# A decoder layer on one core: identity matmuls at the start, another order of the down-projection's units, a layer norm's root by tokens, and a planner with two transfer queues

## The chip, the core and the metric

The kernel runs on one core of a Trainium2 chip. The time is device microseconds (us) of one execution. The engines are called as the profile calls them: PE (TensorE, the matmuls) with PEld (its weight loads), DVE (VectorE), ACT (ScalarE), POOL (GpSimd) and SP (SyncE). Each has an instruction stream of its own that is worked off in order. SP and POOL serve here only to issue transfers: SP plain loads and stores, POOL those that add to what is already in the buffer.

## The reference

One layer over 512 tokens of width 1024, in f32, with 256 memory tokens, a feed-forward width of 2816, and a final norm:

```python
h = _rmsnorm(x, norm_mix_g)
gb, gc, v, u, ug, q, p_g = split(h @ w_in)           # widths 1024 each, p_g 3072
y_a = (gb * conv3(gc * v)) @ w_a_out
u = conv31(u * sigmoid(ug)) + conv_b_bias
y_b = silu(layernorm(u, ln_b_g, ln_b_b)) @ w_b_out
y_c = attention(q, rmsnorm(mem) @ w_kv) @ w_att_out  # 4 heads of 256
g = sigmoid(p_g + b_gate)                            # one gate for each branch and channel
x = x + (g[0] * y_a + g[1] * y_b + g[2] * y_c) @ w_o
gt, up = split(conv3(_rmsnorm(x, norm_ffn_g) @ w_up))
x = x + (silu(gt) * up) @ w_down
out = _rmsnorm(x, norm_final_g)
```

The layer norm's variance is the mean over the 1024 channels of the squared, centred values, and its root scales each token.

## The kernel before

**Products.** Each f32 operand is split on the chip into a high half (a cast on ACT, `whi` for weights, line 405) and a low half (the rest, a subtraction on DVE, `wlo`, line 409), and each product is three matmuls: high by high, high by low, low by high. One low half of the merge's weights is made another way: ACT writes the negated high half and POOL adds the weight to it by a transfer (line 422). The names of buffers in the rows carry numbers that only tell them apart.

**Projections.** The in- and the up-projection are done in quads, two by two blocks multiplied with seven products instead of eight. A quad loads four weight blocks u, v, s, r (SP, line 431). Products 1, 2 and 4 use loaded blocks; 5, 6, 7 and 3 use sums of blocks, which POOL forms by accumulating transfers of 512 KB into the buffers s and u once the product that used their older content has been split (line 532, jobs `s5`, `s6`, `s7`, `s3`). The activations have forms of their own for these products (`ft5`, `ft6`, `ft7`, `fb11` and so on, an ACT cast at line 497 and a DVE subtraction at line 502). The matmuls of all quads stand at line 574, and the PE takes them in a fixed order.

**Start.** The memory's keys and values come first (line 794). The PE waits there for the memory's tokens (`mh`, `ml`) and the first weights.

**Layer norm of branch B.** `acc` holds the convolved channels with tokens along the free axis, 512 columns. The squares of the centred values are added into one buffer of two 512-wide halves. Before, these were split in parts, two matmuls with a matrix of 1/1024 gave the variance on all 128 partitions, ACT took the root of 128x512 and DVE its reciprocal (line 1178). Then `lns` multiplies `acc` by it (line 1185), ACT applies the gain and silu (line 1192), and the result is split into `ybh` and `ybl` (lines 1202, 1206) for the merge of branch B.

**Down-projection.** It is again seven products, here named a, b, d, c, e, f, g, over 11 pairs of channels in six units each (five of two pairs and one of one pair). So `a4` is the fifth unit of product a. A unit of two pairs is 12 steps on the PE of 512 columns (lines 364 to 366). The right operands are `z`, the gated up-projection, in forms of which ACT makes the high half `zh` (line 1632) and DVE the low half `zl` (line 1639), one for each two units. The weights are loaded blocks for a and b, sums with a further block for e, and running sums in the buffers `x_sum` (for f) and `y_sum` (for d, c and g). The products a, c, e and g add up in one chain of two PSUM banks, so before the first unit of c, e or g, DVE has read the banks into the rows `x` (`read`, line 1770); b, d and f have banks of their own. The rows `x` are the layer's input to this block, kept in DRAM (`x1_kept`) and loaded again during the down-projection. a0 to a2 stand between the last products of the up-projection.

**Order.** A planner (`Jobs`) emits the instructions. Its job list for the PE is in program order. For ACT, DVE and transfers it simulates costs written by hand, and takes next what can start first, and among those what is due first. A job's due time follows from the PE's order, shifted for some kinds of job by the table LATER; the table AHEAD keeps some kinds from running too early. Before, all transfers of SP and POOL share one simulated engine, DMA. Buffers sit in rings: four for split weights of each kind, six for loads. The order that comes out is what each engine then works off; the real times are the chip's.

Of the kernel before, what the change touches and what calls it, by code (L numbers as in the profile page):

```python
# [11 lines left out]
ALU = mybir.AluOpType  # L12
# [45 lines left out]
SOON = 8.0  # L58
SEEN = {"PE": 0.2, "ACT": 0.14, "DVE": 0.12}
# [14 lines left out]
    "ACT wh up 1": 10, "DMA keep": 20, "DVE kl": 80, "DVE zs d": 10,  # L74
# [21 lines left out]
class Jobs:  # L96
# [6 lines left out]
    def __init__(self, rings):  # L103
        self.jobs, self.place, self.left = {}, {}, {}
        self.rings = {r: {i: 0.0 for i in range(n)} for r, n in rings.items()}

# [69 lines left out]

    def run(self, log=None):
# [15 lines left out]
        while n:  # L193
# [40 lines left out]
            ends[key] = start + cost + latency  # L234
# [16 lines left out]
def hybrid_block_kernel(  # L251
# [86 lines left out]
    LOAD, MORE, MORE_WIDE = 1.5, 2.9, 2.9  # L338
    LOAD_LATENCY, MORE_LATENCY = 2.3, 3.0
# [50 lines left out]
    def split_job(unit, key, n_k, n, after, wide=None, lo_from=None):  # L390
# [22 lines left out]
        def define():  # L413
# [14 lines left out]
    def fetch_job(key, src, cost=LOAD, after=(), take=("wf",)):  # L428
        def fetch():
            t = make(key)  # L430
            nc.sync.dma_start(out=t[:, : src.shape[1]], in_=src)

        job(("ld", key), "DMA", cost, fetch, after, LOAD_LATENCY, take=[(key,) + take])
# [92 lines left out]
    def quad_loads(q, w, col0, col1, by_dma=False, take=("wf",), after=()):  # L526
# [12 lines left out]
        job(("s5", q), "DMA", MORE, lambda: more(s, 1, 1), [("ld", s)], MORE_LATENCY, use=[s])  # L539
        split_job((q, 5), s, 4, 256, [("s5", q)])  # L540
        if by_dma:
            deferred.append(lambda: job(
                ("s6", q), "DMA", MORE, lambda: more(s, 0, 0), [("wl", (q, 5))], MORE_LATENCY,
                use=[s]))
        else:
# [6 lines left out]
            ("s7", q), "DMA", MORE, lambda: more(u, 1, 0), [("wl", (q, 1))] + ([] if by_dma else [("s6", q)]),  # L552
# [3 lines left out]
            ("s3", q), "DMA", MORE, lambda: more(s, 0, 1), [("wl", (q, 6))], MORE_LATENCY,  # L556
# [89 lines left out]
    R_MEM, R_X, SS_X, ATT = column(0, MC), column(2, NT), 6, 12  # L646

    for g in range(2):
        for e in range(2):
# [9 lines left out]
            job(("ldm", g, e), "DMA", 0.85, load_mem, [("ldm", g, 0)] if e else [], 2.4,  # L659
# [43 lines left out]
    def squares_to_tokens(bank, key, n, width):  # L703

        ps, sq = make(bank), tiles[key]
        for c in range(n):
            for j in range(0, 1024, width):
                nc.tensor.matmul(
                    ps[:, c : c + 1], sq[:, j + c * P : j + (c + 1) * P], mean_col,
                    start=j == 0, stop=j + width == 1024,  # L710
                )
# [110 lines left out]
    for p in range(4):  # L822
# [7 lines left out]
        job(("ldx", p), "DMA", 1.6, load_x, [("ldm", 1, 1)], 2.4, take=[(("x", p), ANY)])  # L830
# [32 lines left out]
    job(("ldp",), "DMA", 0.3, lambda: nc.sync.dma_start(  # L863
        out=pk[:, N_GAINS:], in_=packed[:, N_GAINS:]), [("ldx", 3)], 2.4)
    scale_jobs("x", R_X, ("ss", "x"), NT)

    def pe_squares(s, key, n, width, after):
        pe((s, "squares"), n * (1024 // width) * 0.22,
           lambda: squares_to_tokens(("ss", s), key, n, width), after,
# [300 lines left out]
    sums_split("var", ("csq", 0))  # L1170

    def var_root():
        make(("rstd",))
        nc.scalar.activation(two(("rstd",))[:, 0, :], tiles["bank", "var"], AF.Sqrt, bias=eps)

    def var_scale():
        t = two(("rstd",))[:, 0, :]
        nc.vector.reciprocal(t, t)
# [145 lines left out]
    for t in range(NT):  # L1324
# [4 lines left out]
        job(("ldr", t), "DMA", 1.6, load_row, late_rows, 2.4, take=[(("x1", t), "sb")])  # L1329
# [5 lines left out]
    job("ldg", "DMA", 1.6, load_gain, late_rows, 2.4, take=[(("gffn",), "sb")])  # L1335
# [86 lines left out]
    for t in range(NT):  # L1422
        for half in range(2):
# [4 lines left out]
        job(("keep", t), "DMA", 1.6, lambda t=t: nc.sync.dma_start(  # L1428
            out=x1_kept[t], in_=tiles["x1", t]), both, 2.4, use=[("x1", t)])
# [66 lines left out]
    NU = len(PAIR_UNITS)  # L1496
    for h in range(HEADS - 1):
# [37 lines left out]
        (GATE[1, 1], 6): lambda: (pe_mean("var"), pe_merge(0, 3, (0,))),  # L1535
        (GATE[1, 1], 7): lambda: pe_merge(0, 3, (1,)),
# [45 lines left out]
    down_order = [("a", 3), ("b", 0), ("b", 1), ("a", 4), ("a", 5)] + [("b", u) for u in range(2, NU)]  # L1582
    down_order += [(p, u) for p in DOWN[2:] for u in range(NU)]
# [58 lines left out]
    for g, ps in enumerate(PIECES):  # L1642
# [3 lines left out]
        for p, at in (("a", (0, 0)), ("b", (0, 1)), ("d", (0, 1)), ("c", (0, 0)), ("e", (0, 0)),  # L1646
# [12 lines left out]
            k = 3 * DOWN.index(p) + g - 3  # L1659
            if k >= 0:  # L1660
                src = src + [("pd", DOWN[k // 3], min(2 * (k % 3) + 1, NU - 1))]
# [23 lines left out]
    def open_rows():  # L1685
# [3 lines left out]
            tc.tile_pool(name="rows1", bufs=8, side="right", reuse_waits="tile")  # L1689
        )  # L1690
        late["x1"] = [
            [pool.tile([P, SEQ], F32, tag="a", name=name("x1")) for _ in range(2)]
            for _ in range(NT)
        ]
# [3 lines left out]
    for t in range(NT):  # L1698
        job(("x1b", t), "DMA", 1.7, lambda t=t: [nc.sync.dma_start(
# [178 lines left out]
```

## Time and profile before

| What | us |
|---|---|
| Median of 3 runs | 960.09 |
| Lowest and highest run | 959.14, 960.75 |
| The profiled execution's own time | 960.77 |
| Its span | 959.0 |
| PE busy | 929.3 (97%) |
| DVE busy | 818.7 (85%) |
| ACT busy | 664.4 (69%) |
| POOL busy | 125.1 (13%) |

The mean granted clock of the PE over the profiled execution is 0.992 of full speed. The span runs from the first to the last instruction of the profiled execution; its own time is 1.8 us longer, as it holds what lies around the span. In rows of the timeline the columns are start, duration, engine, source line and operation, output and inputs, sizes, and in brackets how long the engine sat idle before and what ended that. In the chain of waits a row is start, length, and the work itself. Matmuls on the PE overlap, so the step from one start to the next is what a matmul costs, not its duration.

### The profile page before, as it was taken

The page shows a single profiled execution, that of the slowest core. Times are in us where ns is not written, and L with a number is a line of the kernel's source. Part 1 is how long each engine was busy: PE and PEld are TensorE (multiplying, and loading weights), DVE is VectorE, ACT ScalarE, POOL GpSimd, SP SyncE. Part 2 cuts the span into 40 slices and gives each one's busy share as a digit, 9 for nine tenths or more (in the row PEclk, how much of TensorE's full clock was granted, in tenths as well). Part 3 has the DMA queues.
Part 4 walks back from the last instruction along what each step waited for, and adds up shares of the span by engine and source line. Part 5 has one row for each costly group of instructions (what it writes and reads, how often), then busy time and mean ns, then how long its engine had stood idle before and what let it go on. Part 6 is the DMA issues. An engine that isn't in the chain of part 4 may idle for free.

```text
span 959.0 us, 16820 instructions
## 1 busy us (share of the span) xinstructions
PE 929.3 (97%) x6736; PEld 872.8 (91%) x6736; DVE 818.7 (85%) x921; ACT 664.4 (69%) x905; POOL 125.1 (13%) x151
## 2 busy tenths in 40 slices
PE   6999999999999999999999999999999999989897
PEld 6999999999989999999897888899999999978685
DVE  5797999999989999999587653687999889998966
ACT  6556987998997986779377431766676667765455
POOL 0011111111021111111110000021211211012300
PEclk9999999999999999999999999999999999999999
DMA  9869879765699869996865644499998977689922
GB/s 356 269 154 257 186 195 205 169 154 111 177 220 249 167 146 224 227 212 198 200 150 142 217 129 113 137 188 316 250 227 224 201 151 159 194 308 311 226 55 88
DMA packets 54959, 188.51 MB, mean 197 GB/s; under 512 B 6113, under 2 KB 7265, under 8 KB 54881
## 3 DMA queue, kind: packets, MB, share of 16 engines
q0 software_dynamic: 20592, 74.20, 43.8%
q1 hardware_dynamic: 34144, 113.23, 33.6%
q8 instruction: 53, 0.87, 0.3%
q14 instruction: 26, 0.20, 0.1%
q10 hardware_dynamic: 144, 0.01, 0.0%
HBM read 183.22 MB, written 4.19 MB: 195 GB/s over the span
## 4 chain that ended last, share of the span: by engine, by line
PE 79%; DVE 8%; DMA 7%; issue 3%; ACT 2%; SPq 0%; POOL 0%; DVEq 0%; POOLq 0%; ACTq 0%
PE bank L574 47%; PE bank L366 5%; PE bank L364 5%; PE bank L365 5%; PE bank L1275 5%; PE bank L1273 5%; PE bank L1274 5%; DVE wlo L409 3%; DMA wf<-in_w_in 3%; DMA wf<-in_w_up 3%; PE bank L794 3%; DMA wlo<-in_w_a_out 1%; DVE zl L1639 1%; DMA wf<-in_w_kv 1%; ACT whi L405 1%
## 5 line engine op out<-in xcount | busy, mean ns | idle before, releaser
L405 ACT CAST whi<-wf 128x1024 fp32r<-128x1024 f32 (+1 forms) x227 | 236.3, 1045 | 153.0 <-PE bank L1274 44.4
L409 DVE TENSOR_TENSOR wlo<-wf,whi 128x1024 fp32r<-128x1024 f32 (+1 forms) x217 | 261.8, 1212 | 53.3 <-ACT whi L405 53.2
L1085 ACT ACTIVATE tp<-u,pk 128x482 f32<-128x482 f32 (+22 forms) x184 | 119.5, 706 | 4.7 <-DVE acc L1092 2.6
L1092 DVE TENSOR_TENSOR acc<-acc,tp 128x1002 f32<-128x1002 f32 (+21 forms) x92 | 109.1, 1188 | 6.5 <-ACT tp L1085 5.0
L532 POOL DMA_DIRECT2D wf<-in_w_in x61 | 53.2, 877 | 282.1 <-DVE wlo L409 215.1
L364 PE MATMUL bank<-whi,zh 128*128 128x512 f32 x154 | 61.3, 398 | 6.0 <-DVE x L1770 3.1
L574 PE MATMUL bank<-ft6h,wlo 128*128 128x256 f32 x232 | 64.4, 278 | 1.5 <-DVE wlo L409 1.5
L574 PE MATMUL bank<-fb00h,wlo 128*128 128x256 f32 x232 | 64.5, 278 | 0.6 <-DVE wlo L409 0.6
L574 PE MATMUL bank<-ft6h,whi 128*128 128x256 f32 x232 | 64.4, 278 | 0.5 <-ACT whi L405 0.5
L574 PE MATMUL bank<-ft7h,whi 128*128 128x256 f32 x232 | 64.5, 278 | 0.1
L574 PE MATMUL bank<-fb10h,whi 128*128 128x256 f32 x232 | 64.5, 278 | 0.0
L574 PE MATMUL bank<-fb00h,whi 128*128 128x256 f32 x232 | 64.4, 277 | 0.0
L574 PE MATMUL bank<-ft7l,whi 128*128 128x256 f32 x232 | 64.4, 277 | 0.0
L574 PE MATMUL bank<-ft7h,wlo 128*128 128x256 f32 x232 | 64.4, 277 | 0.0
L574 PE MATMUL bank<-fb00l,whi 128*128 128x256 f32 x232 | 64.3, 277 | 0.0
L574 PE MATMUL bank<-fb11h,whi 128*128 128x256 f32 x232 | 64.3, 277 | 0.0
L574 PE MATMUL bank<-ft5h,whi 128*128 128x256 f32 x232 | 64.3, 277 | 0.0
L574 PE MATMUL bank<-ft5l,whi 128*128 128x256 f32 x232 | 64.3, 277 | 0.0
L574 PE MATMUL bank<-ft5h,wlo 128*128 128x256 f32 x232 | 64.3, 277 | 0.0
L574 PE MATMUL bank<-ft6l,whi 128*128 128x256 f32 x232 | 64.2, 277 | 0.0
L574 PE MATMUL bank<-fb11h,wlo 128*128 128x256 f32 x232 | 64.2, 277 | 0.0
L574 PE MATMUL bank<-fb10h,wlo 128*128 128x256 f32 x232 | 64.2, 277 | 0.0
(344 smaller groups left out, 3094.6 us busy)
## 6 DMA issues: line engine op xcount, KB each, us to landing
wf<-in_w_in SPq DMA_DIRECT2D x62, 512.0 KB, 5.7
wf<-in_w_in POOLq DMA_DIRECT2D x61, 512.0 KB, 6.3
wf<-in_w_up POOLq DMA_DIRECT2D x31, 512.0 KB, 6.6
wf<-in_w_up SPq DMA_DIRECT2D x30, 512.0 KB, 4.9
wf<-in_w_kv SPq DMA_DIRECT2D x16, 512.0 KB, 7.6
wf<-in_w_down SPq DMA_DIRECT2D x15, 512.0 KB, 4.3
wf<-in_w_att_out SPq DMA_DIRECT2D x8, 512.0 KB, 3.7
wf<-in_w_a_out SPq DMA_DIRECT2D x8, 512.0 KB, 4.1
```

What stands on the lines that cost most here:

```text
L364: nc.tensor.matmul(ps, s_hi, w_hi, start=start, stop=False, skip_group_check=again)
L365: nc.tensor.matmul(ps, s_hi, w_lo, start=False, stop=False, skip_group_check=again)
L366: nc.tensor.matmul(ps, s_lo, w_hi, start=False, stop=stop, skip_group_check=again)
L405: nc.scalar.copy(parts[0], src())
L409: nc.vector.tensor_tensor(lo, src(), hi.bitcast(F32), op=ALU.subtract)
L532: nc.gpsimd.dma_start(out=tiles[key], in_=block(w, col[c], k), accum_op=ALU.add)
L574: nc.tensor.matmul(ps[:, c, :], w[:, k, at], a[k], start=first and n == 0, stop=i == 3 and n == 2, skip_group_check=again,)
L1085: nc.scalar.activation(two(("tp", p, s))[:, j, s:], two(("u", p))[:, j, : SEQ - s], AF.Copy, scale=weight(j),)
L1092: nc.vector.tensor_tensor(a, a, two(("tp", p, s))[:, :, s:], op=ALU.add)
L1273: nc.tensor.matmul(ps, w_hi[:, i, at], hi, start=first, stop=False)
L1274: nc.tensor.matmul(ps, w_hi[:, i, at], lo, start=False, stop=False)
L1275: nc.tensor.matmul(ps, w_lo[:, i, at], hi, start=False, stop=last)
```

## The change

It has six parts.

**Identity matmuls.** The PE's program begins with 14 matmuls of the 128x128 identity with itself into a bank that nothing reads.

**Down order.** Before: a3, b0, b1, a4, a5, b2 to b5, then all of d, c, e, f, g. After: a3, b0, b1, b2, a4, b3, a5, b4, b5, all of d, all of c, f0 to f3, all of e, f4, f5, g. The release of a form's buffers (`down_pieces`, `piece_end`) follows the new order.

**Layer norm's root.** The two halves of the squares are added on DVE (`fold`). Four f32 matmuls with one column (`pe_squares`, after unit 6 of the last gate of branch B) give each token's variance on 128 partitions by 4 columns. ACT and DVE take root and reciprocal there, and four transposes (`pe_rows`, after unit 7) spread them along tokens in a bank, which `lns` reads.

**Planner.** Transfers of SP and of POOL are two queues, which share the bandwidth 0.3 to 0.7 while both have work (`transfer_end`); some costs and latencies of transfers and the two tables are other ones.

**Reload of the rows.** `x1_kept` comes back in four transfers of 512 KB instead of eight of 256 KB.

**Last stores.** The two halves of a tile are issued from ACT and SP instead of both from SP.

```diff
+SHARE = 0.3
...
 LATER = {
-    "ACT rh": 32, "ACT wh up 1": 6, "ACT wh up 2": 48, "DMA ea": 11, "DMA keep": 5.5,
+    "ACT fh h2 t4": 1, "ACT r1 gate": 169, "ACT rb": 248, "ACT wh mix 7": 0.5, "ACT wh up 4": 309,
...
+    def transfer_end(self, queue, start, cost):
+        work, t = self.work, self.at
+        share = {"SP": SHARE, "POOL": 1.0 - SHARE}
...
+        self.at = start
+        work[queue] += cost
+        mine, other = work[queue], work["POOL" if queue == "SP" else "SP"]
+        if other == 0.0:
+            return start + mine
+        both = min(mine / share[queue], other / (1.0 - share[queue]))
+        return start + both + mine - both * share[queue]
...
             fn()
             free[e] = start + cost
-            ends[key] = start + cost + latency
+            if e in self.work:
+                free[e] = self.transfer_end(e, start, cost)
+            ends[key] = free[e] + latency
...
-    LOAD, MORE, MORE_WIDE = 1.5, 2.9, 2.9
-    LOAD_LATENCY, MORE_LATENCY = 2.3, 3.0
+    LOAD, MORE, MORE_WIDE = 1.45, 2.4, 2.4
+    LOAD_LATENCY, MORE_LATENCY = 2.6, 3.6
...
-        job(("s5", q), "DMA", MORE, lambda: more(s, 1, 1), [("ld", s)], MORE_LATENCY, use=[s])
+        job(("s5", q), "POOL", MORE, lambda: more(s, 1, 1), [("ld", s)], MORE_LATENCY, use=[s])
...
-    sums_split("var", ("csq", 0))
...
-    job("vroot", "ACT", actv(512), var_root, [("var", "mean")], take=[(("rstd",), ANY)],
-        use=[("bank", "var")])
-    job("vscale", "DVE", 3.26, var_scale, ["vroot"], use=[("rstd",)])
+    job(("var", "fold"), "DVE", dve(512), lambda: fold(("csq", 0)), [("var", "sum")],
+        use=[("csq", 0)])
+    scale_jobs("v", R_V, ("ss", "v"), NT)
...
-            two(("acc", p)), two(("acc", p)), on_both(two(("rstd",))[:, 0, :]), op=ALU.mult),
-            ["vscale"], use=[acc, ("rstd",)])
+            two(("acc", p)), two(("acc", p)), on_both(tiles["rows", "v"]), op=ALU.mult),
+            [("v", "rows")], use=[acc, ("rows", "v")])
...
+    def warm_up():
+        ps = make(("bank", "warm"))
+        for i in range(14):
+            nc.tensor.matmul(ps[:, :P], ident, ident, start=True, stop=True)
+
+    pe(("warm",), 6.0, warm_up, take=[(("bank", "warm"), "ps")], unit=False)
...
-        (GATE[1, 1], 6): lambda: (pe_mean("var"), pe_merge(0, 3, (0,))),
-        (GATE[1, 1], 7): lambda: pe_merge(0, 3, (1,)),
+        (GATE[1, 1], 6): lambda: (
+            pe_squares("v", ("csq", 0), NT, SEQ, [("var", "fold")], SEQ), pe_merge(0, 3, (0,))),
+        (GATE[1, 1], 7): lambda: (pe_rows("v", R_V, NT), pe_merge(0, 3, (1,))),
...
-    down_order = [("a", 3), ("b", 0), ("b", 1), ("a", 4), ("a", 5)] + [("b", u) for u in range(2, NU)]
-    down_order += [(p, u) for p in DOWN[2:] for u in range(NU)]
+    down_order = [("a", 3), ("b", 0), ("b", 1), ("b", 2), ("a", 4), ("b", 3), ("a", 5)]
+    down_order += [("b", 4), ("b", 5)] + [(p, u) for p in "dc" for u in range(NU)]
+    down_order += [("f", u) for u in range(4)] + [("e", u) for u in range(NU)]
+    down_order += [("f", u) for u in range(4, NU)] + [("g", u) for u in range(NU)]
...
-        job(("x1b", t), "DMA", 1.7, lambda t=t: [nc.sync.dma_start(
-            out=late["x1"][t][i], in_=x1_kept[t, :, i * 512 : (i + 1) * 512]) for i in range(2)],
-            ["rows"], 2.4)
+        job(("x1b", t), "SP", LOAD, lambda t=t: nc.sync.dma_start(
+            out=late["row"][t], in_=x1_kept[t]), ["rows"], LOAD_LATENCY)
...
-        for i in (1, 0):
-            nc.sync.dma_start(
-                out=out[t * P : (t + 1) * P, i * 512 : (i + 1) * 512], in_=x1[i]
-            )
+        for i, queue in ((1, nc.scalar), (0, nc.sync)):
+            queue.dma_start(out=out[t * P : (t + 1) * P, i * 512 : (i + 1) * 512], in_=x1[i])
```

Three places show how instructions move.

ACT, in the first quads of the up-projection, before (an operation, its output and input; `ft5h`, `ft7h`, `ft6h` are high halves of activation forms, `whi` of weights, `uu` a copy of a finished bank):

```order
L497 CAST ft5h_6972<-h_892_6940 128x1024
L497 CAST ft7h_6977<-h2b_6841 128x1024
L497 CAST ft6h_7008<-h2b_6703 128x1024
L405 CAST whi_7039<-wf_6455 128x1024
L405 CAST whi_7043<-wf_6556 128x1024
L604 COPY uu_7050<-bank_7012 128x2x256
```

And after:

```order
L524 CAST ft5h_6994<-h_895_6991 128x1024
L524 CAST ft7h_7025<-h2b_6870 128x1024
L432 CAST whi_7030<-wf_6544 128x1024
L524 CAST ft6h_7059<-h2b_6735 128x1024
L432 CAST whi_7063<-wf_6473 128x1024
L432 CAST whi_7068<-wf_6901 128x1024
```

The cast of an accumulated weight stood behind that of `ft6h` and now stands ahead of it.

DVE, at the end of product c of the down-projection, before (`wlo` from `y_sum` is a low half for c, from `wf` for e; line 370 forms a sum of z; line 1770 reads the bank of chain a):

```order
L409 TENSOR_TENSOR wlo_9893<-y_sum,whi_9892 128x1024
L409 TENSOR_TENSOR wlo_9899<-y_sum,whi_9898 128x512
L1639 TENSOR_TENSOR zl_9918<-z,zh_9903 128x1024
L370 SCALAR_TENSOR_TENSOR z<-z 128x4x256
L370 SCALAR_TENSOR_TENSOR z<-z 128x3x256
L409 TENSOR_TENSOR wlo_9921<-wf_9799,whi_9920 128x1024
L1639 TENSOR_TENSOR zl_9951<-z,zh_9938 128x1024
L1770 TENSOR_TENSOR x_1200_9596<-x_1200_9596,bank_9330 128x512
L1770 TENSOR_TENSOR x_1202_9598<-x_1202_9598,bank_9334 128x512
```

And after (`wlo` from `x_sum` is a low half for f; the lines 436, 1672, 397 and 1800 are the former 409, 1639, 370 and 1770):

```order
L1672 TENSOR_TENSOR zl_9930<-z,zh_9900 128x1024
L436 TENSOR_TENSOR wlo_9933<-y_sum,whi_9932 128x512
L436 TENSOR_TENSOR wlo_9925<-x_sum,whi_9924 128x1024
L436 TENSOR_TENSOR wlo_9949<-x_sum,whi_9948 128x1024
L1672 TENSOR_TENSOR zl_9966<-z,zh_9953 128x1024
L436 TENSOR_TENSOR wlo_9964<-x_sum,whi_9963 128x1024
L436 TENSOR_TENSOR wlo_9985<-x_sum,whi_9984 128x1024
L397 SCALAR_TENSOR_TENSOR z<-z 128x4x256
L436 TENSOR_TENSOR wlo_10003<-wf_9764,whi_10002 128x1024
L1800 TENSOR_TENSOR x_1199_9625<-x_1199_9625,bank_9354 128x512
```

The four low halves for f and their forms of z now stand between c's last low half and e's first one, and the read of c's bank comes after them.

POOL, in the middle of the up-projection, before (each row is an accumulating transfer; a buffer appears once for each of its sums):

```order
L532 DMA ('up', 3)_936_7318<-in_w_up 128x1024
L532 DMA ('up', 3)_924_7183<-in_w_up 128x1024
L532 DMA ('up', 4)_945_7362<-in_w_up 128x1024
L532 DMA wf_7632<-in_w_up 128x1024
L532 DMA ('up', 4)_957_7498<-in_w_up 128x1024
```

And after:

```order
L559 DMA ('up', 3)_927_7205<-in_w_up 128x1024
L559 DMA wf_7457<-in_w_up 128x1024
L559 DMA ('up', 3)_919_7166<-in_w_up 128x1024
L559 DMA ('up', 4)_933_7275<-in_w_up 128x1024
L559 DMA wf_7619<-in_w_up 128x1024
```

The first sum into a later quad's buffer (`wf_7632` before, `wf_7457` after) stood behind the last sum into quad 3's buffer `s` (7183 before, 7166 after) and now stands ahead of it.

More of the change, by code (lines that the diff above doesn't have):

```diff
@@ L66 @@
 LATER = {
[4 rows of a table removed]
[4 rows of a table added]
 }
 AHEAD = {
-    "ACT wh up 1": 10, "DMA keep": 20, "DVE kl": 80, "DVE zs d": 10,
+    "ACT fh h2 t4": 5, "ACT r5 gate": 20, "ACT sigmoid": 10, "ACT tap 1": 150, "ACT wh mix 7": 5,
+    "DVE r2 bb": 5, "SP ld b 0": 10, "SP ld up v": 20,
 }
@@ L175, in free_places @@
         return sorted(own + (other if len(other) > leave else []), reverse=True)
+    def transfer_end(self, queue, start, cost):
+        work, t = self.work, self.at
+        share = {"SP": SHARE, "POOL": 1.0 - SHARE}
+        while t < start and (work["SP"] > 0.0 or work["POOL"] > 0.0):
+            both = work["SP"] > 0.0 and work["POOL"] > 0.0
+            rate = share if both else {"SP": 1.0, "POOL": 1.0}
+            step = min([start - t] + [work[q] / rate[q] for q in work if work[q] > 0.0])
+            for q in work:
+                work[q] -= rate[q] * step if work[q] > 0.0 else 0.0
+                if work[q] < 1e-9:
+                    work[q] = 0.0
+            t += step
+        self.at = start
[5 more added lines that the diff above has]
+        return start + both + mine - both * share[queue]
     def run(self, log=None):
@@ L431, in fetch @@
             nc.sync.dma_start(out=t[:, : src.shape[1]], in_=src)
-        job(("ld", key), "DMA", cost, fetch, after, LOAD_LATENCY, take=[(key,) + take])
+        job(("ld", key), "SP", cost, fetch, after, LOAD_LATENCY, take=[(key,) + take])
     def unit_job(unit, src, n_k=4, lo_by_dma=False):
@@ L542, in quad_loads @@
             deferred.append(lambda: job(
-                ("s6", q), "DMA", MORE, lambda: more(s, 0, 0), [("wl", (q, 5))], MORE_LATENCY,
+                ("s6", q), "POOL", MORE, lambda: more(s, 0, 0), [("wl", (q, 5))], MORE_LATENCY,
                 use=[s]))
@@ L551, in quad_loads @@
         deferred.append(lambda: job(
-            ("s7", q), "DMA", MORE, lambda: more(u, 1, 0), [("wl", (q, 1))] + ([] if by_dma else [("s6", q)]),
+            ("s7", q), "POOL", MORE, lambda: more(u, 1, 0), [("wl", (q, 1))] + ([] if by_dma else [("s6", q)]),
             MORE_LATENCY, use=[u]))
@@ L555, in quad_loads @@
         deferred.append(lambda: job(
-            ("s3", q), "DMA", MORE, lambda: more(s, 0, 1), [("wl", (q, 6))], MORE_LATENCY,
+            ("s3", q), "POOL", MORE, lambda: more(s, 0, 1), [("wl", (q, 6))], MORE_LATENCY,
             use=[s]))
@@ L701, in hybrid_block_kernel, with squares_to_tokens @@
         [("msq", 0), ("msq", 1)], use=[("msq", 0), ("msq", 1)])
-    def squares_to_tokens(bank, key, n, width):
+    def squares_to_tokens(bank, key, n, width, total=1024):
         ps, sq = make(bank), tiles[key]
         for c in range(n):
-            for j in range(0, 1024, width):
+            for j in range(0, total, width):
                 nc.tensor.matmul(
                     ps[:, c : c + 1], sq[:, j + c * P : j + (c + 1) * P], mean_col,
-                    start=j == 0, stop=j + width == 1024,
+                    start=j == 0, stop=j + width == total,
                 )
@@ L1688, in open_rows @@
         pool = ctx.enter_context(
-            tc.tile_pool(name="rows1", bufs=8, side="right", reuse_waits="tile")
+            tc.tile_pool(name="rows1", bufs=NT, side="right", reuse_waits="tile")
         )
[L1691 to L1694, printed above, removed]
+        late["row"] = [pool.tile([P, D], F32, tag="a", name=name("x1")) for _ in range(NT)]
+        late["x1"] = [[t[:, i * 512 : (i + 1) * 512] for i in range(2)] for t in late["row"]]
     job("sums", "NONE", 0.0, open_sums, [(q, f) for q in UP for f in range(1, 8)])
```

52 lines of the change are left out of this document (26 added, 26 removed), and 6 rows, old and new, of the table LATER.

## Prediction

> **What bounds the kernel now.** I read the page's busy times first, then the busy time of stretches, then the waits of the PE, then the timeline at the long waits.
>
> ```profile
> PE 929.3 (97%) x6736; PEld 872.8 (91%) x6736; DVE 818.7 (85%) x921; ACT 664.4 (69%) x905; POOL 125.1 (13%) x151
> ```
>
> The PE is busy for 929.3 of 959.0 us. So 29.7 us at most can be won by feeding it better, and a little more by keeping its clock up. The same table by stretches (width, then busy time and count of each engine, then granted clock, DMA share, GB/s) shows where those 29.7 lie:
>
> ```profile
> 0.00:10.00 10.00, 2.34 (x7) 1.72 (x7) 3.65 (x6) 6.17 (x11) 0.77 (x8) 1.00 0.83 270
> 500.00:550.00 50.00, 47.65 (x252) 40.84 (x251) 33.36 (x33) 32.05 (x38) 0.86 (x1) 0.97 0.61 190
> 600.00:650.00 50.00, 47.77 (x345) 44.48 (x344) 37.01 (x43) 33.62 (x51) 6.95 (x8) 1.00 0.71 167
> 650.00:700.00 50.00, 47.40 (x407) 46.62 (x407) 43.96 (x51) 34.60 (x44) 9.57 (x11) 1.00 1.03 284
> 700.00:750.00 50.00, 50.00 (x443) 50.00 (x442) 44.10 (x51) 32.86 (x42) 9.60 (x11) 1.00 0.90 212
> 850.00:900.00 50.00, 45.86 (x194) 36.68 (x193) 45.75 (x49) 26.38 (x31) 14.45 (x17) 0.97 1.05 311
> 900.00:920.00 20.00, 16.85 (x68) 13.48 (x67) 14.55 (x15) 10.08 (x11) 1.23 (x2) 0.91 0.92 182
> 950.00:959.00 9.00, 2.18 (x10) 1.48 (x8) 2.52 (x5) 3.02 (x8) 0.00 (x0) 0.74 0.47 180
> ```
>
> Width less PE busy: 7.7 us idle at the start, 2.4 at 500, 2.2 and 2.6 in the up-projection's first quads, 4.1 and 3.2 in the down-projection, 6.8 after the last product; 700 to 750 has none. The waits of the PE name them (total, times, longest):
>
> ```profile
> PE bank L794 <- ACT whi L405: 6.2, 1, 6.2
> PE bank L364 <- DVE x L1770: 3.1, 1, 3.1
> PE bank L364 <- ACT zh L1632: 2.9, 1, 2.9
> PE bank L1275 <- DMA wlo<-in_w_a_out: 2.4, 1, 2.4
> PE bank L574 <- DVE wlo L409: 2.1, 3, 0.8
> PE bank L365 <- DVE wlo L409: 1.2, 1, 1.2
> ```
>
> **The change part by part.** Terms stand against the profiled execution's own 960.77 us; it is 0.68 above the median of 960.09, which I take off at the end.
>
> **Identity matmuls.** The chain of waits gives the memory products twice, at two speeds, and the timeline gives the identity's end, the first product and the last one before an unbroken row:
>
> ```profile
> 10.92 7.26 PE bank L794 x41
> 25.94 5.76 PE bank L794 x48
> 1.02 0.29 POOL masks.py:199 TENSOR_SCALAR_AFFINE_SELECT ident<-ident 128x128 f32<-128x128 f32 x1
> 6.23 0.58 PE L794 MATMUL bank<-mh,whi 128*128 128x256 f32 x1 [6.23 <-ACT whi L405]
> ```
>
> A product takes 7.26/41 = 0.177 us first and 5.76/48 = 0.120 later, so the slow start costs 41 x 0.057 = 2.3 us. The added matmuls can begin at 1.31, when the identity is made. An f32 matmul of width 128 should cost about one or two such products: 14 to 28 x 0.177 = 2.5 to 5.0 us, so they end by 6.3 and lie in the 6.23 wait. Their own cost is nothing; if that cover fails, the idle time up to 10.92 still holds them. What they bring lies between 0 and -2.3, since the PE idles again before 10.92. This kernel shows how little idle time brings the slow pace back:
>
> ```profile
> 506.23 0.50 PE L1275 MATMUL bank<-yah,wlo 128*128 128x512 f32 x1 [2.35 <-DMA wlo<-in_w_a_out]
> 510.69 0.40 PE L1275 MATMUL bank<-yah,wlo 128*128 128x512 f32 x1
> ```
>
> The 12 steps between these rows take 4.46 us; at 0.227 a step they would take 2.72, so 2.35 us of idle cost 1.7 more. I take half of the start's bound, -1.2. [...]
>
> **Layer norm's root by tokens.**
>
> ```profile
> 18.18 1.68 PE ss L708 x16
> 506.01 3.35 DVE L1178 RECIPROCAL rstd<-rstd 128x512 f32<-128x512 f32 x1 [4.45 <-ACT rstd L1174]
> 520.38 2.35 DVE L1206 TENSOR_TENSOR ybl<-acc,ybh 128x1024 fp32r<-128x1024 f32 x2
> 526.79 0.39 PE L1273 MATMUL bank<-ybh,whi 128*128 128x512 f32 x1
> ```
>
> The DVE loses the 3.35 us reciprocal, but it ends 4 us ahead of use (520.38 + 2.35 = 522.73 against 526.79). The PE gains 8 narrow passes for the squares, of the kind that took 1.68/16 = 0.105 each, and 4 transposes, put at the same price: 12 x 0.105 = 1.26. It loses two 512-wide products (0.45): +0.8. Both stand ahead of the product that waits 2.35 us for the weight's low half at 506.23, so that wait, whose transfer is issued at the same place, hides them. The multiplications by the root move behind the transposes, after one more unit on the PE, some 6 us later by the order, and eat the 4 us lead and the 3.35 won: about 1 us is left. I take 0; ends are +0.8 (cover gone) and -4.1 (the 2.35 wait and its 1.7 slow steps both vanish).
>
> **First up quads.** The ACT order above puts the cast of an accumulated weight ahead of that of ft6:
>
> ```profile
> 633.83 1.05 ACT L497 CAST ft6h<-h2b 128x1024 fp32r<-128x1024 f32 x1 [1.22 <-DVE h2b L370]
> 637.97 1.05 ACT L405 CAST whi<-wf 128x1024 fp32r<-128x1024 f32 x1 [2.13 <-DMA wf<-in_w_up]
> 639.05 1.23 DVE L409 TENSOR_TENSOR wlo<-wf,whi 128x1024 fp32r<-128x1024 f32 x1 [1.25 <-ACT whi L405]
> ```
>
> Its product starts when wlo is there, at 640.28. With the casts exchanged, ft6h ends at 637.97 + 2 x 1.05 = 640.07, and its low half a DVE operation later (1.23), at 641.3: +1.1 us. Ends are +5 (each of four quads so) and -4.8 (the 2.2 and 2.6 idle both go).
>
> **Down order.** The first fence holds the two long waits and the first product after each at full pace; the second the DVE's load and its one long wait.
>
> ```profile
> 855.16 0.65 PE L364 MATMUL bank<-whi,zh 128*128 128x512 f32 x1 [2.89 <-ACT zh L1632]
> 858.91 0.39 PE L366 MATMUL bank<-whi,zl 128*128 128x512 f32 x1
> 905.45 0.47 PE L364 MATMUL bank<-whi,zh 128*128 128x512 f32 x1 [3.15 <-DVE x L1770]
> 910.09 0.39 PE L365 MATMUL bank<-wlo,zh 128*128 128x512 f32 x1
> ```
>
> ```profile
> 840.00:905.30 65.30, 58.16 (x258) 47.04 (x256) 60.94 (x67) 37.23 (x45) 15.68 (x18) 0.97 1.01 290
> 870.76 0.69 DVE L1770 TENSOR_TENSOR x<-x,bank 128x512 f32<-128x512 f32 x1 [3.71 <-DMA x<-x_kept]
> ```
>
> At 855.16 unit a4 waits 2.89 us for the last z, then 8 steps take 3.75 instead of 1.81: 1.9 slow. Unit b2, now ahead of it, is 12 steps of 0.227 = 2.7 us of work that needs no late z. It fills the gap and keeps the clock: -2.7 - 1.9 = -4.6. At 905.45 unit e0 waits 3.15 for the read of chain a's bank, and 13 steps take 4.64 instead of 2.95: 1.7 slow. Units f0 to f3 write another bank and are 48 steps, 10.9 us, so that read is covered: -4.85. The 1.2 us wait for a low half (line 365) lies in c and goes too if the DVE is not later: -1.2.
>
> What is late next is the DVE itself, 60.94 of 65.30 us busy. By the order above, the z and weight halves of f0 must now be there where e0's were, but ahead of them stand five DVE operations fewer (about 5.5 us at 1.1 each). It had finished for e0 at 905.3, so for f0 it is done at 899.8, or 4.2 earlier (895.6) if its 3.71 wait for the kept rows and the rest of its 4.36 idle shrink away. The PE ends c 2.7 + 1.9 + 1.2 = 5.8 us earlier than before (905.45 - 3.15 = 902.3), so it comes at 896.5 and waits 0 to 3.3. I take 1.4, nearer the lower end, since the first read now stands four operations later on the DVE and finds its rows landed. Part: -4.6 - 4.85 - 1.2 + 1.4 = -9.25, between -10.7 (no wait for the DVE) and 0 (b2 and f0 as late as a4 and e0 were).
>
> **Stores and reloads.** Two stores of a tile are issued one behind the other in 0.81 us:
>
> ```profile
> 954.97 0.81 SPq L1801 DMA_DIRECT2D out<-x  x2
> ```
>
> Issued on ACT and SP at once, the second leaves half of that earlier: -0.4 (ends 0 and -0.8). Reloads of x1 become four of 512 KB; their cost is the DVE wait priced above.
>
> **Two counted queues elsewhere.** Between 700 and 750 the PE has no idle time, so another order of SP and POOL can win nothing there: 0.
>
> Sum: -1.2 + 0 + 1.1 - 9.25 - 0.4 = -9.75. From 960.77 that is 951.0; less 0.68, **950.3 us** against the median. About 0.2%, 1.9 us, is what a measurement of this kernel can tell from no change.
>
> **Rivals.** *More goes* (0.15): the new queue order also ends the waits at 503 (4.1) and in the first up quads (4.8, and my +1.1 does not come): 10 us more, 940.3. For it: both are waits for transfers or what hangs on them. Against: the accumulating transfer at 503 keeps its place, and the ACT order got worse.
>
> *The DVE takes it back* (0.10): its idle time in 840 to 905.3 is 4.36, so with a full 3.7 wait at the kept rows and c's low halves late, the down part gives half, 4.4: 960.1 - 1.2 + 1.1 - 4.4 - 0.4 = 955.2. For it: its load; against: fewer operations ahead of f0.
>
> *No effect* (0.07): the clock falls back before 10.92 (0), and b2 only moves the wait to b's later units, as the DVE stays the bound: 959 to 961.
>
> *Slower* (0.10): POOL issues in order, and its order now has the first accumulation of a later quad ahead of the second or third of an earlier one in some 19 places. A late load then holds both:
>
> ```profile
> 655.40 0.86 POOL L532 DMA_DIRECT2D ('up', 3)_924_7183<-in_w_up  x1 [3.24 <-DMA ('up', 3)_924_7183<-in_w_up]
> 663.69 1.22 DVE L409 TENSOR_TENSOR wlo<-wf,whi 128x1024 fp32r<-128x1024 f32 x1
> 666.74 0.28 PE L574 MATMUL bank<-fb11h,whi 128*128 128x256 f32 x1
> ```
>
> POOL waited 3.24 us for a load; the low half of the next accumulated weight ended (663.69 + 1.22 = 664.91) 1.83 us ahead of its use. Such a stall behind a quad costs 3.24 - 1.83 = 1.4. At 7 places it eats the 9.75; at 10 of 19 the time is 950.3 + 14 = 964.3. Against it: loads normally lead by far more.
>
> **How the numbers follow.** My forecast has 0.58. Faster is forecast, more, and the DVE's: 0.83; same 0.07; slower 0.10. The range must leave out no more than 0.2: it runs from just above the case of more (941) to the near edge of no effect (959).
>
> **What the changed profile would show.** Identity matmuls inside the first 6.3 us and products from 10.92 at 0.12: right; 0.177 again: that term is 0. No wait of a4 on zh and no granted clock under 0.97 between 850 and 920: right; a wait on the DVE at f0 above 3 us, or at c: the DVE took it. PE idle in 600 to 700 above 5 us with POOL waiting for loads: the slower rival. The wait near 503 gone: that of more. The forecast fails if the new order opens waits between 60 and 480, which I priced at nothing.

## The result and the profile after

The changed kernel took 953.95 us in the median of 4 runs (953.10 to 955.23) beside 960.42 for the kernel before; the ratio is 0.9935, with an interval of 0.9918 to 0.9952. It is 6.5 us faster; 950.3 was forecast, 9.8 us less than before. The profiled execution took 953.81 us, its span 951.9, 7.1 less than before.

The page's line of busy times, the table by stretches and the waits of the PE, all of the changed kernel, answer to those shown of before:

```profile
PE 931.3 (98%) x6774; PEld 877.3 (92%) x6774; DVE 812.9 (85%) x920; ACT 666.7 (70%) x905; POOL 124.8 (13%) x151
```

```profile
0.00:10.00 10.00, 6.39 (x30) 6.00 (x30) 2.38 (x5) 4.87 (x8) 0.77 (x8) 1.00 0.73 242
500.00:550.00 50.00, 47.67 (x265) 41.50 (x264) 31.01 (x32) 33.80 (x40) 1.73 (x2) 0.93 0.59 179
600.00:650.00 50.00, 48.22 (x335) 44.39 (x334) 34.88 (x41) 30.86 (x48) 6.93 (x8) 1.00 0.70 170
650.00:700.00 50.00, 46.48 (x405) 45.91 (x404) 43.00 (x51) 34.69 (x44) 10.44 (x12) 1.00 1.04 283
840.00:905.30 65.30, 65.30 (x310) 54.75 (x309) 65.16 (x69) 41.12 (x48) 14.78 (x17) 1.00 0.97 284
900.00:920.00 20.00, 20.00 (x90) 16.57 (x89) 17.77 (x18) 11.44 (x12) 2.54 (x3) 1.00 1.05 207
```

```profile
PE bank L601 <- DVE uu L397: 2.5, 1, 2.5
PE bank L1293 <- DMA wlo<-in_w_a_out: 2.3, 1, 2.3
PE bank L821 <- ACT whi L432: 2.1, 1, 2.1
PE bank L601 <- ACT g L631: 0.8, 1, 0.8
PE bank L601 <- DVE ft6l L529: 0.8, 1, 0.8
PE bank L601 <- DVE B L397: 0.7, 1, 0.7
```

The waits of the down-projection are gone: between 840 and 905.3 the PE has no idle time at all, and the DVE beside it has 0.14 us of it. The wait near 506 stands as it was, and three of the others are new.

Of the 6.39 us that the PE is busy in the first 10 us, 5.89 are the identity, which says nothing about progress. A better reading compares when the same product starts in both traces. The PE's program is the same but for the parts that the change touches, so a product of the quads can be counted: the first, and the 2201st, 2601st, 3001st and 3801st of the 4872 at line 574 (601 after). From their starts follow the stages:

| Stage, until | before, us | after, us | difference | forecast |
|---|---|---|---|---|
| first quad product | 51.01 | 52.26 | +1.25 | -1.2 |
| 2201st (383 before) | 332.20 | 332.34 | +0.14 | 0 |
| 2601st (429) | 45.45 | 47.40 | +1.95 | 0 |
| 3001st (524), with the layer norm | 95.41 | 96.77 | +1.36 | 0 |
| 3801st (714), with the first up quads | 189.65 | 188.82 | -0.83 | +1.1 |
| first step of the down-projection | 113.57 | 113.58 | 0 | 0 |
| last step of the down-projection | 124.50 | 113.17 | -11.33 | -9.25 |
| end of the span | 7.21 | 7.56 | +0.35 | -0.4 |

The differences add up to the span's 7.1. The down order brought more than all of it, and 4.2 us were given back elsewhere. One trace of each kernel stands behind the table. How far a row repeats is shown by e8 and e12 below, which are one and the same program: their down-projections took 113.16 and 113.05 us, but their stages with the layer norm 95.78 and 94.75, and with the first up quads 188.60 and 190.73. So the row of the down-projection is clear of this, and the others, of 0.1 to 2 us, are near what one program shows twice.

### The profile page after: what moved, and what is told of

Its sections match the earlier page's. It is cut to its first block, busy times and chain, and to the rows that moved or that the text cites. A ratio compares the mean times of both kernels' runs of the same rounds, so it can differ in the third digit from the quotient of the medians.

```text
span 951.9 us, 16901 instructions
## 1 busy us (share of the span) xinstructions
PE 931.3 (98%) x6774; PEld 877.3 (92%) x6774; DVE 812.9 (85%) x920; ACT 666.7 (70%) x905; POOL 124.8 (13%) x151
## 4 chain that ended last, share of the span: by engine, by line
PE 82%; issue 6%; DMA 5%; DVE 4%; ACT 1%; POOL 0%; SPq 0%; ACTq 0%; POOLq 0%; DVEq 0%
PE bank L601 49%; PE bank L393 5%; PE bank L391 5%; PE bank L392 5%; PE bank L1293 5%; PE bank L1292 5%; PE bank L1291 5%; PE bank L821 3%; DMA wf<-in_w_up 2%; DMA wf<-in_w_in 1%; DVE wlo L436 1%; DMA wlo<-in_w_a_out 1%; DMA wf<-in_w_kv 1%; ACT whi L432 1%; PE bank L1041 0%
## 5 line engine op out<-in xcount | busy, mean ns | idle before, releaser
L432 ACT CAST whi<-wf 128x1024 fp32r<-128x1024 f32 (+1 forms) x211 | 219.3, 1043 | 145.8 <-PE bank L601 38.5
L436 DVE TENSOR_TENSOR wlo<-wf,whi 128x1024 fp32r<-128x1024 f32 (+1 forms) x201 | 242.5, 1212 | 59.2 <-ACT whi L432 58.4
L1112 ACT ACTIVATE tp<-u,pk 128x510 f32<-128x510 f32 (+22 forms) x184 | 119.8, 706 | 9.0 <-DVE acc L1119 8.8
L1119 DVE TENSOR_TENSOR acc<-acc,tp 128x1020 f32<-128x1020 f32 (+22 forms) x92 | 109.0, 1188 | 9.2 <-ACT tp L1112 7.5
L559 POOL DMA_DIRECT2D wf<-in_w_in x50 | 43.9, 877 | 244.5 <-DVE wlo L436 175.3
L601 PE MATMUL bank<-fb10l,whi 128*128 128x256 f32 x232 | 64.2, 277 | 0.0
L601 PE MATMUL bank<-fb11l,whi 128*128 128x256 f32 x232 | 64.1, 276 | 0.0
```

The source lines that it names most:

```text
L432: nc.scalar.copy(parts[0], src())
L436: nc.vector.tensor_tensor(lo, src(), hi.bitcast(F32), op=ALU.subtract)
L559: nc.gpsimd.dma_start(out=tiles[key], in_=block(w, col[c], k), accum_op=ALU.add)
L601: nc.tensor.matmul(ps[:, c, :], w[:, k, at], a[k], start=first and n == 0, stop=i == 3 and n == 2, skip_group_check=again,)
L1112: nc.scalar.activation(two(("tp", p, s))[:, j, s:], two(("u", p))[:, j, : SEQ - s], AF.Copy, scale=weight(j),)
L1119: nc.vector.tensor_tensor(a, a, two(("tp", p, s))[:, :, s:], op=ALU.add)
```

## The experiments

**One half, both halves, and the former order.** e1 is the kernel before with the new order of the down units alone and the release of the forms' buffers that goes with it (the dots).

```diff
-    down_order = [("a", 3), ("b", 0), ("b", 1), ("a", 4), ("a", 5)] + [("b", u) for u in range(2, NU)]
-    down_order += [(p, u) for p in DOWN[2:] for u in range(NU)]
+    down_order = [("a", 3), ("b", 0), ("b", 1), ("b", 2), ("a", 4), ("b", 3), ("a", 5)]
+    down_order += [("b", 4), ("b", 5)] + [(p, u) for p in "dc" for u in range(NU)]
+    down_order += [("f", u) for u in range(4)] + [("e", u) for u in range(NU)]
+    down_order += [("f", u) for u in range(4, NU)] + [("g", u) for u in range(NU)]
...
```

> The kernel before with the new order of the down units alone (and the release of the forms' buffers that goes with it); planner, tables and everything else are those of before. Theory: the order itself carries the gain, since it puts work without late inputs under the two long waits; the ledger of the two traces gives 11.3 us between the start of a0 and that of g0, so the time is 949 to 951 (ratio 0.989 to 0.990). Rival: the order needs the new tables and queues, because the old tables deliver the halves for f0 where they delivered those for e0; then c or f0 waits 4 us or more for the DVE and the time is 954 to 957.

Measured: 954.21 us beside 959.32, ratio 0.9947 (0.9928 to 0.9966). From the first to the last down step it took 116.64 us instead of 124.50. The theory's 949 to 951 was too low: 7.9 of the 11.3 us come with the order alone. The time is in the rival's range, but its wait of 4 us or more at c or f0 is not there: this profile lost 2.9 us earlier, in the first up quads (192.55 us instead of 189.65), where the granted clock is 0.83 between 660 and 680. The PE's waits from 825 on in e1 are one group, on the DVE's low halves:

```profile
PE bank L365 <- DVE wlo L409: 2.3, 3, 1.3
```

e2 is the changed kernel with the former order (the diff above, turned round).

> The changed kernel with the former order of the down units. Theory: the waits at a4 and e0 and their slow steps come back, 9 to 11.5 us, so 963 to 965.5, slower than before, since the rest of the change costs about 4 us. Rival: the new tables alone already removed part of the waits in the down part; then less than 7 us come back and the time is below 961.

Measured: 978.24 us, ratio 1.0205 (1.0188 to 1.0222), and a down-projection of 138.34 us. Neither theory has such a time. One wait of the PE is new, and ACT and SP show its cause (a wait of the PE, then a row of ACT and one of SP):

```profile
PE bank L391 <- ACT whi L432: 16.5, 1, 16.5
```

```profile
876.93 0.62 ACT L432 CAST whi<-wf 128x512 fp32r<-128x512 f32 x1 [19.18 <-DMA wf<-in_w_down]
859.78 18.86 SPq L458 DMA_DIRECT2D wf<-in_w_down  x5
```

A small unit's weight was loaded behind the blocks of the sums and the kept rows on SP and landed at 876.9, while the PE stood. So e2 does not price the order: under the new planner the former order puts one load in the wrong place.

The next three separate this. e9 and e10 are the kernel before with one half of the order each; e11 is the changed kernel, with the start order of e3 below, with the second half alone. Of each order the new lines are shown.

```diff
 # e9
+    down_order = [("a", 3), ("b", 0), ("b", 1), ("b", 2), ("a", 4), ("b", 3), ("a", 5)]
+    down_order += [("b", 4), ("b", 5)] + [(p, u) for p in DOWN[2:] for u in range(NU)]
 # e10 and e11
+    down_order = [("a", 3), ("b", 0), ("b", 1), ("a", 4), ("a", 5)] + [("b", u) for u in range(2, NU)]
+    down_order += [(p, u) for p in "dc" for u in range(NU)]
+    down_order += [("f", u) for u in range(4)] + [("e", u) for u in range(NU)]
+    down_order += [("f", u) for u in range(4, NU)] + [("g", u) for u in range(NU)]
...
```

> The kernel before with only the first half of the new order: b2 ahead of a4 and b3 ahead of a5, then all of d, c, e, f, g as before. From the first to the last step of the down-projection the kernel before takes 124.5 us and e1, with both halves, 116.6. Theory: b2 fills the wait at a4 and saves its slow steps, 2.9 + 2.0; the wait at e0 stays: 119.5 to 120.5. Rival: DVE, earlier loaded, is what holds the part, so that the wait only moves to e0; then 123 or more.

> The kernel before with only the second half of the new order: f0 to f3 ahead of e, f4 and f5 behind it. Theory: the wait for the read of chain a's bank and the slow steps after it go, 3.2 + 1.7, less what the low halves for c and f cost because DVE is late, some 1 to 2: from the first to the last step 120.5 to 121.5 instead of 124.5. Rival: without b2 the a4 wait of 2.9 gives DVE the time to be ready for f, and the whole 6 go: 118.5. If DVE takes all of it back: 124.

> e3 with only the second half of the new order (a4 and a5 where they were, f0 to f3 ahead of e), with the loads of a and b ahead of those of the sums as in the changed kernel. Theory: the stall of 16 us in e2 came from one load of a weight that stood behind the sums' loads on SP, not from the order of the products itself; so here only the wait at a4 with its slow steps is back: 117.5 to 119 from first to last step instead of 113.1, and 954 to 956 in all. Rival: the new tables cannot serve the former place of a4 at all; then 125 or more and 961 or more.

Measured, from the first to the last down step: e9 122.83, e10 119.23, e11 118.04 us. In time, e9 was 960.20 beside 958.44 (ratio 1.0019, 0.9999 to 1.0038), e10 957.54 (0.9987, 0.9967 to 1.0007), e11 956.50 (0.9983, 0.9960 to 1.0006). These ratios hardly tell the kernels apart, and the stage is what is read. The PE's waits of the down-projection in e9, e10 and e11, in this order:

```profile
PE bank L365 <- DVE wlo L409: 4.2, 4, 2.0
PE bank L364 <- DVE x L1775: 1.0, 1, 1.0
```

```profile
PE bank L365 <- DVE wlo L409: 2.3, 3, 1.1
PE bank L364 <- ACT zh L1639: 2.1, 1, 2.1
PE bank L366 <- DVE zl L1646: 0.4, 1, 0.4
```

```profile
PE bank L391 <- ACT zh L1665: 2.5, 1, 2.5
PE bank L393 <- DVE zl L1672: 0.4, 1, 0.4
```

In e9 the rival holds but for 0.2 us, not the theory: b2 removes the wait at a4, and the DVE takes most back, with late low halves (4.2 us) rather than at e0 (1.0). So b2 alone is worth 1.7 us under the former planner, and 2.6 where f0 to f3 stand ahead of e (119.23 in e10, 116.64 in e1). In e10 the whole is 5.3, between theory and rival. In e11 the theory holds for the stage (the whole, 956.50, is 0.5 above its range): without the stray load, only the wait at a4 is back, and b2 is worth 118.04 - 113.04 (e3) = 5.0 us. So the gain of 11.5 in e3's down-projection is 5.0 for b2 and 6.5 for the rest, and with the new planner both halves bring 3.6 more than with the former one (113.04 instead of 116.64). That its order of the DVE does this is argued, not shown: e1 and e3 also differ in the reload of the rows, and no run takes the two apart. For the DVE's order speaks that the PE's only waits in e1 are for low halves, and that the DVE's wait for the kept rows is gone in e1 and e9 too, which have the former reload.

**The start.** In the changed kernel SP loads the memory's two halves first, and the first weight is cast 3 us later than before (ACT of the kernel before, then of the changed one; then the changed one's identity matmuls, the PE's wait for its first product, two rows of its chain of waits, and its stretch from 10 to 20):

```profile
5.14 1.04 ACT L405 CAST whi<-wf 128x1024 fp32r<-128x1024 f32 x1 [0.37 <-DMA wf<-in_w_kv]
```

```profile
8.23 1.04 ACT L432 CAST whi<-wf 128x1024 fp32r<-128x1024 f32 x1 [2.86 <-DMA wf<-in_w_kv]
1.36 5.89 PE L1519 MATMUL bank<-ident 128*128 128x128 f32 x28 [1.36 <-POOL ident masks.py:199]
9.32 0.39 PE L821 MATMUL bank<-mh,whi 128*128 128x256 f32 x1 [2.07 <-ACT whi L432]
12.22 7.20 PE bank L821 x41
27.18 5.76 PE bank L821 x48
10.00:20.00 10.00, 9.21 (x54) 8.92 (x54) 7.97 (x10) 7.60 (x11) 0.00 (x0) 0.66 1.03 414
```

The first product takes 0.39 us, where it was 0.58, but the 41 products from 12.22 on take 0.176 us each again, and the granted clock is 0.66 there. They also start 1.3 us later than before (12.22 instead of 10.92), which is all of the stage's +1.25. (The granted clock does not show every slow start: in the kernel before it reads 1.00 from 10 to 20, with 0.177 us for each of the same products.) e3 removes the entry of the planner's table that put the weights back, which restores the order memory, weight, memory, weight; e4 leaves one identity matmul.

```diff
 # e3
-    "DVE rd f": 48, "DVE tap 3": 24.5, "DVE wl up 1": -200, "SP ld K 0": 3, "SP ld a 0": 37,
+    "DVE rd f": 48, "DVE tap 3": 24.5, "DVE wl up 1": -200, "SP ld a 0": 37,
 # e4 (and, on e3, e6)
-        for i in range(14):
+        for i in range(1):
```

> The changed kernel without one entry of the table LATER, that for the first key weight loads; SP then loads memory, weight, memory, weight as before instead of memory twice, then weights. Theory: the late first weight (cast at 8.23 instead of 5.14) is what the start lost, so the first products begin near 6.3 and the whole is 1.2 to 2.5 us faster than the changed kernel: 951.5 to 952.8; with the identity matmuls up to 7.2 the first of them run at full pace. Rival: the start is bound by the memory's tokens and by the slow pace after any idle time; then the products still reach full pace only near 16 to 17 and the time is that of the changed kernel, 953.5 to 954.5.

> The changed kernel with one identity matmul instead of 14, in the same order of all else. Theory: the pace falls back in the idle time between 7.25 and 12.2 anyway, so the products after 12.2 take 0.21 us each up to about 16 to 17 with or without them: within 0.6 us of the changed kernel, 953.4 to 954.6. Rival: the identity matmuls save some slow steps, and without them it is 1 to 2 us slower, 955 to 956.

> e3 with one identity matmul instead of 14. Theory: with the first weight early, the PE still idles between 8.7 and 10.9, the pace falls back after it, and the identity matmuls only move the slow stretch; within 0.8 us of e3's 950.3. Rival: with the weights early the identity matmuls do pay, and without them the time is 1.2 to 2.3 us longer, 951.5 to 952.6.

Measured: e3 950.31 us beside 959.32, ratio 0.9910 (0.9896 to 0.9923); e4, measured together with it, 953.20, 0.9933 (0.9916 to 0.9950), beside the changed kernel's 0.9935; e6 952.63 beside 959.27, 0.9928 (0.9910 to 0.9947), where e3's and e6's intervals overlap. So e3 is 2.9 us below e4 by the medians, with intervals that just overlap, and one identity matmul instead of 14 makes no difference that can be told. e3 is 1.2 us below its theory's range and e4 0.2 below its own. e6 lies at the upper end of its rival's range, so a gain of some 2 us from the identity matmuls with early weights is not excluded; against it stands e12 below, with 14 of them, the start of e3 and a ratio of 0.9941. The chains of e3, e4, e6 and e7 (below, with 14), at the same 41 products, show why a trace does not settle it:

```profile
10.94 7.71 PE bank L821 x41
```

```profile
11.96 6.08 PE bank L821 x41
```

```profile
10.49 7.63 PE bank L821 x41
```

```profile
10.77 5.22 PE bank L821 x41
```

Start and length added, the 41 products end at 18.7, 18.0, 18.1 and 16.0. With 14 identity matmuls the pace falls back in e3 and not in e7. e8 and then e12, one and the same program with the start of e3, show it once more (the 41 products, and the stretch from 10 to 20):

```profile
10.87 6.63 PE bank L821 x41
10.00:20.00 10.00, 9.13 (x66) 9.13 (x66) 7.94 (x11) 7.43 (x10) 0.00 (x0) 0.83 1.04 415
```

```profile
10.78 5.21 PE bank L821 x41
10.00:20.00 10.00, 9.22 (x77) 9.22 (x78) 7.75 (x11) 6.72 (x9) 0.00 (x0) 1.00 1.02 411
```

It is not the program that decides this. But e3's profile gained at the start only 0.77 us of the 3.6 by which its span is below the changed kernel's (52.26 to 51.49 at the first quad product); another 2.4 came between the 2601st and the 3001st product, where its wait for the low half was 1.0 instead of 2.3. That the start order alone gives the 2.9 us is therefore not shown.

**The wait at the layer norm.** The changed kernel's PE, from the squares to the transposes:

```profile
505.56 0.95 PE L735 MATMUL ss<-mean_col,csq 128*128 128x1 f32 x8
509.40 0.80 PE L1293 MATMUL bank<-yah,wlo 128*128 128x512 f32 x1 [2.33 <-DMA wlo<-in_w_a_out]
515.40 0.40 PE L1292 MATMUL bank<-yal,whi 128*128 128x512 f32 x1
520.05 0.60 PE L744 MATMUL rows<-ident,cols 128*128 128x128 f32 x4
```

The stretch at half the clock behind that wait, in the kernel before and in the changed one:

```profile
507.20:510.61 3.41, 3.41 (x10) 2.66 (x9) 3.41 (x3) 0.00 (x0) 0.00 (x0) 0.50 0.93 197
508.39:515.21 6.82, 5.81 (x14) 4.57 (x15) 1.23 (x1) 1.05 (x1) 0.00 (x0) 0.50 0.59 172
```

It is 3.41 us longer, and half of that, 1.7 us, is lost.

e5 is e3 with the low half of the weight that the PE waits for at 509.40 made by DVE.

```diff
-                unit_job(("merge", br, m, g), block(W_OUT[br], m * 256, g), lo_by_dma=br != 1 and 2 * m + g > 2)
+                unit_job(("merge", br, m, g), block(W_OUT[br], m * 256, g), lo_by_dma=br != 1 and 2 * m + g > 2 and (br, m, g) != (0, 3, 0))
```

> The changed kernel with the start order of e3, and with the low half of the one merge weight for which the PE waited near 506 to 510 made by DVE from the loaded block instead of by an accumulating transfer. Theory: the wait of 1.0 to 2.3 us and the slow steps after it (8 to 12 of about 0.2 us too much) go, since DVE is busy only 31 of 50 us there; 2.5 to 5 us faster than e3's 950.3, so 945.5 to 948. Rival: that wait only stands in for something later, such as the last form of branch B or the next weights, and the time stays within 1 us of e3.

Measured: 951.34 us, ratio 0.9906 (0.9883 to 0.9929), no gain over e3. The wait is gone and its stage is 91.91 us instead of e3's 94.42, as the theory had it. (e6, which keeps a wait of 1.2 us there but shows a granted clock of 1.00, has 92.95.) But the next stage, to the 3801st product, is 191.43 instead of 188.58: all of the 2.5 and a little more is given back. In e5 a stretch of it shows a lower clock (the table by stretches), and the PE waits for `uu` as in the changed kernel:

```profile
660.00:680.00 20.00, 17.50 (x137) 17.34 (x136) 17.70 (x21) 14.54 (x18) 3.96 (x5) 0.91 1.06 270
```

```profile
PE bank L601 <- DVE uu L397: 2.5, 1, 2.5
```

A clock of 0.91 over 20 us is 1.8 us. That the edit causes this is not shown: e4, e6 and e7 make that low half by the transfer and took 191.4 to 191.9 us for the stage, with the same 0.91, and e8 and e12, one program, took 188.60 at 1.00 and 190.73 at 0.91. So e5 shows that the wait can be removed and is worth up to 2.5 us in its own stage; whether the next stage takes it back, as the rival has it, stays open.

e7 is e3 with the former root (split sums, two matmuls, root and reciprocal on 128x512).

> e3 with the former way to the layer norm's root: two matmuls of the split sums, root and reciprocal on 128x512. Theory: the PE saves 0.8 for the squares and 0.35 for the transposes and spends 0.45, so 0.4 to 1.1 us faster than e3 if nothing else waits, 949.2 to 949.9. Rival: the 3.35 us reciprocal on DVE and the root on ACT hold the multiplications up so far that branch B's first form is late; then 1 to 3 us slower than e3, 951.3 to 953.3.

Measured: 949.99 us, ratio 0.9908 (0.9887 to 0.9930), the same as e3 and 0.1 us above the theory's range; the rival's 1 to 3 us did not come. Its stage is 95.33 us beside e3's 94.42, but its wait for the low half was 2.9, not 1.0. The difference between the two roots is below what this can tell.

**The stores.** e8 and e12 are one kernel: e3 with both last stores on SP, run once as e8 and seven times as e12.

```diff
-        for i, queue in ((1, nc.scalar), (0, nc.sync)):
-            queue.dma_start(out=out[t * P : (t + 1) * P, i * 512 : (i + 1) * 512], in_=x1[i])
+        for i in (1, 0):
+            nc.sync.dma_start(
+                out=out[t * P : (t + 1) * P, i * 512 : (i + 1) * 512], in_=x1[i]
+            )
```

> e3 with both last stores of a tile on SP as before; read from the profile, since the difference is too small for the times. Theory: the stores that ACT issued (0.37 us each) stood ahead of the next tile's scaling; without them the last read of the bank comes some 0.4 us earlier after the last matmul, and the second store of the last tile is issued 0.4 later, so from the last matmul to the end of the span within 0.15 us of the changed kernel's. Rival: the second queue does bring the issue forward and nothing else moves, and the end comes 0.4 us later than with two queues.

> The kernel of e8 (start order of e3, both last stores on SP), timed. Theory: the profiles give 0.4 to 0.6 us less from the last matmul to the end than with two queues, so 949.5 to 950.2, the fastest version here; rival: no difference to e3 that can be measured, 950.3 and its interval. Either way about 9 us below the kernel before.

Measured: from the last step to the end of the span e8 took 7.0 us and e12, the same program, 7.6, as the changed kernel did; the time was 950.14 in e8's one run and 952.75 in the median of e12's seven, beside 958.44, ratio 0.9941 (0.9919 to 0.9963). My theory from e8 does not stand: this stage varies by 0.6 us in one and the same kernel, more than either way of storing could bring. e12 differs from e3 in the stores alone and has a ratio 0.3% higher, with intervals that just overlap; so much is also the doubt about e3's 0.9910. Whether the second queue helps stays open.

## Why the prediction was right or wrong

The time lay in the range, and faster was right. That the total came so near, 6.5 us faster after a forecast of 9.8, is in part luck: two stages came out about 2 us better than forecast each, and four others 0.8 to 2.5 worse. The range was also drawn too narrow by its own chances: the cases that it leaves out, of more (0.15), no effect (0.07) and slower (0.10), come to 0.32, not 0.2. By steps:

- **Down order: right mechanism, too small.** Forecast -9.25, measured -11.33. Both waits and their slow steps went, and the step that failed is the 1.4 us for a late DVE: the DVE has 65.16 busy of 65.30 us without holding the PE. Its wait of 3.71 for the kept rows is gone. e9 shows how near this was, since with the former planner the DVE did take back 3.3 of b2's 5.0 us. The other 0.7 us lie beyond the better end that I gave (-10.7); what they are is not shown.
- **Identity matmuls: no gain.** Forecast -1.2, measured +1.25. By the sign that I had named, products at 0.177 us again, the term is 0. Two steps failed. The cover held only because the first weight came late: 28 passes took 5.89 us where I had 2.5 to 5.0, ended at 7.25 and not by 6.3, and with the weights early, in e8, the high half of the first weight is there at 6.46 and the first product starts behind the identity only at 7.36. And the step counted a first weight at its old time: I had not followed SP's order ahead of the first product, and it had put the weight 3 us back. That this loses 1.25 us is one trace's word: with the loads late the stage took 50.9 to 52.3 us (e4, e2, the changed kernel), with the start of the kernel before 50.7 to 52.2 (e9, before, e1, e10), and with the loads early and 14 identity matmuls 48.8 to 51.5 (e7, e11, e8, e12, e3, e5). The lapse of the pace, my reason to take half, did come, at 12.2. It did not come alike in two executions of one program: the 41 products took 6.63 us in e8 and 5.21 in e12.
- **Layer norm's root: the cover held, the price did not.** The squares (0.8) were hidden: the wait was 2.33 after 2.35. But behind it the 14 steps from 509.40 to 515.40 took 6.00 us, 2.8 more than at the 0.229 of the steps from 515.40 to 517.00, where it had been 1.7, and the transposes stood uncovered with 0.35. The stage is 1.36 longer instead of 0, no more than the 1.7 of the longer stretch at half the clock. The waits do not order the clocks behind them in these traces: between 500 and 550 the granted clock is 0.93 in the changed kernel after a wait of 2.33 and 0.97 in the kernel before after one of 2.35, 0.97 in e3 after a wait of 1.0, and 1.00 in e9 after one of 1.8.
- **First up quads: wrong in sign.** The wait for ft6's low half came (0.8 us) and that for `uu` grew from 1.3 to 2.5, but those for `wlo` shrank from 2.1 to 0.8, and the stage is 0.83 shorter. Over the fourteen traces it took 188.6 (e3) to 192.55 us (e1), so it varies by more than the term.
- **Two queues elsewhere: 0 was wrong.** Between the 2201st and the 2601st product the changed kernel is 1.95 slower, with waits for `B` and `g` (0.7 and 0.8 us) that were not there; the same stage takes 46.2 to 47.95 us in the ten traces with the new planner, and 45.4 to 45.6 in the four with the former one (the kernel before, e1, e9, e10). I had said that new waits there would make the forecast fail, and gave them no price.
- **Stores:** forecast -0.4, measured +0.35, and not to be told from no change.
- **The rivals:** the sign of the slower rival did show, its cost did not. The PE's idle time between 600 and 700 is 5.3 us after 4.8, and POOL waited there for transfers into its buffers three times, 9.0 us in all, instead of once, 3.2 (its waits in the changed kernel):

```profile
POOL wf L559 <- DMA wf<-in_w_up: 7.0, 2, 4.0
POOL ('up', 4)_933_7275 L559 <- DMA ('up', 4)_933_7275<-in_w_up: 2.0, 1, 2.0
```

The PE's waits there are for DVE and ACT (`uu`, `ft6l`, `wlo`, `whi`), and the stage is shorter, so the 1.4 us a place that I had put on this did not come. Of the case of more, the wait near 503 could be removed (e5), but no gain in time came with it. The DVE did not take the gain back, and of no effect only the lapse of the pace came true.

## What to carry to other kernels

Filling a wait on the PE with work whose inputs are ready paid here only as far as the next engine kept up: with b2 ahead of a4 the down-projection was 1.7 or 2.6 us shorter under the former planner and 5.0 under the new one, beside which the DVE no longer held the PE. Before pricing added work that hides in a first wait, check that the work that ends that wait still starts when it did. When a planner makes the order, a change of one part moves loads of others, so an undone part can cost far more than the part is worth (in e2 one wait of 16.5 us, where the order had brought 11.3); read the stage, not only the total.

## What was not expected of the hardware

In e8 and e12, two executions of one program, the PE's pace after idle time differs: it idled 0.4 to 1.1 us at a time before the same 41 products, which took 6.63 us in one profile and 5.21 in the other, with granted clocks of 0.83 and 1.00 between 10 and 20 us. Between 660 and 680 it was the other way round, 1.00 in e8 and 0.91 in e12, and the first up quads took 188.60 and 190.73 us. So 1.4 us in the one stretch and 2.1 in the other differ with nothing changed in the program, in executions of 950.14 and 952.75 us.
